# Recurrence stage of a two-block network: each head group's Gram, inverse and scan steps issued by a readiness rule, without fill products, with half of the masks on another engine

## The chip, the cores and the metric

The kernel runs on one NeuronCore of a Trainium2 chip. The core has a matrix engine (TensorE, PE in the rows; PEld is its weight load), a vector engine (VectorE, DVE), an activation engine (ScalarE, ACT), a general engine (GpSimd, POOL), and a DMA issuer (SyncE, SP). Each engine runs its own queue in order; semaphores join them. The metric is the device time in microseconds (us), lower is better; one profiled execution gives the trace.

## The reference, cut to what matters

A first block (conformer mixer and conv FFN) is followed by two layers with FFNs; the first of these layers mixes with a delta-rule recurrence (RWKV-7) over 256 positions, 12 heads of 64 channels. The change is in that mixer alone.

```python
def rwkv7_mix(z_in, mu, w0, w_up, a0, a_up, g_up, k_k, k_a, r_k, lnx_g, lnx_b):
    z = token_shift(z_in, mu)              # p + (prev - p) * mu
    ...
    def step(state, inp):
        r_t, w_t, k_t, v_t, kk_t, b_t = inp
        sa = jnp.einsum('bhij,bhj->bhi', state, kk_t)
        state = (state * w_t[:, :, None, :] - sa[..., :, None] * b_t[..., None, :]
                 + v_t[..., :, None] * k_t[..., None, :])
        return state, jnp.einsum('bhij,bhj->bhi', state, r_t)
    ...
    out = ((out - m) * lax.rsqrt(var + LNX_EPS)).reshape(bsz, seq, c) * lnx_g + lnx_b
    bonus = jnp.sum(r * k * r_k, axis=-1, keepdims=True) * v
    y = (out + bonus.reshape(bsz, seq, c)) * g
```

## The kernel before, in words

Weights stream through a ring: SP loads `wraw`, ACT rounds it to a high part `whi` (line 226), DVE takes the low part `wlo` (line 235), and PE multiplies by both. Layers of the network follow one another on PE with little between them.

The class `Rwkv` works in two parts. `project` (line 1441) computes the projections on PE while side tasks prepare decays and keys; a planner (`weave`) orders its steps by costs written in the code. `shifted` (line 1427) applies the token shift to a projection in PSUM by two DVE instructions, the first into a padded tile `mpad`, the second adding the scaled projection: it is called 18 times on projections of the groups and twice at the start. The last projections are the values `v` (`aa`), two column blocks for each of three head groups (4 heads each).

`groups` (line 1630) then treats the three head groups g = 0, 1, 2 in a fixed order, written out by loops:

- *Gram*: for each g and q (two halves), 16 products of keys with queries go to two PSUM banks (line 1667), and DVE multiplies each bank (128x512) by a mask into `G` (line 1671); then for each g three opening steps on DVE make the first inverse factors: `Y` (line 1677, twice), `Z` (1679), `D` (1680, a transpose).
- *Sides*: for each g, v is turned by 8 products with the identity (line 1688, copied by ACT into `vu`, 1690), the keys `kb` are turned by 8 transposes (line 1695, copied by ACT back, 1696), POOL multiplies the bonus by v (`ys`, 1699) and ACT adds a bias (1701).
- *Inverse*: five levels; at each level one set of 16 64x64 products for each g (helper `each`, line 1711) goes to `Y` by a DVE mask (1718), then a second set for each g goes to `D` (1726) and by a transpose to `Z` (1727); at the last level to `Z` alone (1730). `each` ends by calling `idle(0.22)`, which issues two fill products (line 1294, a 128x256 product of the current weight with itself, result unused).
- *Scan*: four chunks c of 64 positions. For each chunk and each g: products into `sc` (`xp`, lines 1746 and 1749), a DVE copy `xs` (1751), products with `Z` (`up`, 1756), results to `vu` by ACT (1758) and DVE (1759), products into `sc` again (`sp`, 1771) from which DVE makes the next state `S` in four instructions (1777 or 1781), with ACT scaling the old state (`sd`, 1768), and the output products `op` (1786, 1790). Each (c, g) ends with two fill products (line 1294).

The PSUM banks come in turn from two pools of three (`ps`): a bank is given out again when its readers are done. After the scan, `hnorm` normalizes the outputs: ACT and DVE copy `op` to `D` (1799 to 1801), products with a centering matrix (1813), two weight products, and 24 products of 2 columns (1822) between them.

The functions that the change touches, with the lines of the profile:

Of the kernel before, what the change touches and what calls it, by code (L numbers as in the profile page):

```python
# [8 lines left out]
F32 = mybir.dt.float32  # L9
# [1383 lines left out]
class Rwkv(Mixer):  # L1393
# [6 lines left out]
    def run(self, li):  # L1400
        b = self.b
        self.n_ps = 0
        self.ready = {}
# [36 lines left out]
    def project(self):  # L1440
        nc, b, mp = self.nc, self.b, self.mp
        self.omm = mp.tile([P, 20], F32, name="omm")
# [6 lines left out]
        self.mpad = [mp.tile([P, T + 1], F32, name=f"mpad{i}") for i in range(4)]  # L1449
        self.n_pad = 0  # L1450
        for t in self.mpad:
            nc.vector.memset(t[:, 0:1], 0.0)
# [13 lines left out]
        self.n_lora, self.n_prep, self.n_val = 0, 0, 0  # L1466
# [20 lines left out]
        for g in range(3):  # L1487
# [8 lines left out]
            self.n_val += 1  # L1496
# [132 lines left out]

    def groups(self):  # L1630

# [3 lines left out]
        ident = b.k("ident")  # L1635
        R = range(3)
        kof, bof = (0, HD), (HD, 0)
        rows = [slice(bof[q], bof[q] + HD) for q in range(2)]
# [7 lines left out]
        G = [gp.tile([P, 2, 2, 4, P], F32, name="G", bufs=2) for _ in range(2)]  # L1646
        G += tiles("G", [2, 2, 4, P], 1)
        Z, D, Y = (tiles(n, [8, HD]) for n in "ZDY")
        vu = tiles("vu", [2, 4, 2, HD])
        for t in vu:  # L1650
            for q in range(2):
                nc.gpsimd.memset(t[rows[q], q], 0.0)
# [3 lines left out]

        mg = b.k("maskg").unsqueeze(1).to_broadcast([P, 4, P])
        for g in R:  # L1660
            ar, kb, _ = self.ready[g]
            for q in range(2):
                gm = [self.ps().rearrange("p (c f) -> p c f", c=4) for _ in range(2)]
                for c in range(4):
                    for h in range(2):
                        r = slice(h * HD, h * HD + HD)
                        mm(gm[h][:, c, :], lhsT=kb[r, 4 * q + c].rearrange("p a t -> p (a t)"),
                           rhs=ar[r, 4 * q + c].rearrange("p a t -> p (a t)"), start=True, stop=True,
                           skip_group_check=True)
                for h in range(2):  # L1670
                    tt(out=G[g][:, q, h], in0=gm[h], in1=mg, op=ALU.mult)

            odd = slice(1, HD, 2)
            zo = Z[g][:, :, odd]
            for q in range(2):
                r = rows[q]
                tt(out=Y[g][r, :, 0:HD // 2], in0=G[g][r, q, :, :, odd].rearrange("p h c t -> p (h c) t"),
                   in1=b.k("m1neg")[r, odd].unsqueeze(1).to_broadcast([HD, 8, HD // 2]), op=ALU.mult)
            tt(out=zo, in0=zo, in1=Y[g][:, :, 0:HD // 2], op=ALU.add)
            nc.vector.transpose(out=D[g], in_=Z[g])  # L1680

        for g in R:
            zv = self.aa[:, 2 * g:2 * g + 2, :]
            vp = [self.ps().rearrange("p (c f) -> p c f", c=4) for _ in range(2)]
            for q in range(2):
                k = slice(kof[q], kof[q] + HD)
                for c in range(4):
                    mm(vp[q][k, c, :], lhsT=zv[:, q, c * HD:c * HD + HD], rhs=ident, start=True,
                       stop=True, skip_group_check=True)
                nc.scalar.copy(out=vu[g][k, q].rearrange("p c h f -> p c (h f)"), in_=vp[q][k])  # L1690
            kbt = self.ready[g][1].rearrange("p i a t -> p i (a t)")
            for q in range(2):
                tp = self.ps()
                for c in range(4):
                    nc.tensor.transpose(tp[:, c * P:c * P + P], in_=kbt[:, 4 * q + c], identity=ident)
                nc.scalar.copy(out=kbt[:, 4 * q:4 * q + 4].rearrange("p c f -> p (c f)"), in_=tp)

            bon = self.sgw[:, 2 * g:2 * g + 2, :]
            nc.gpsimd.tensor_tensor(out=bon, in0=bon, in1=zv, op=ALU.mult)
            for q in range(2):  # L1700
                nc.scalar.activation(out=bon[:, q, :], in_=bon[:, q, :], func=AF.Identity,
                                     bias=b.vec("rwkv_lnx_b_2", 2 * g + q))
        self.b.mark("inv")

        def each(f):

            o = self.ps().rearrange("p (i t) -> p i t", i=8)
            for i in range(8):
                for q in range(2):
                    lhsT, rhs = f(rows[q], q, i)  # L1710
                    mm(o[rows[q], i, :], lhsT=lhsT, rhs=rhs, start=True, stop=True,  # L1711
                       skip_group_check=True)
            self.idle(self.FILL)
            return o
        for s in LEVELS:
            for g in R:
                yp = each(lambda r, q, i: (G[g][r, q, i // 4, i % 4, 0:HD], D[g][r, i, :]))
                tt(out=Y[g], in0=yp, in1=b.k(f"low{s}").unsqueeze(1).to_broadcast([P, 8, HD]),
                   op=ALU.mult)
            for g in R:  # L1720
                if s < 32:
                    dp = each(lambda r, q, i: (Z[g][r, i, :], Y[g][r, i, :]))

                    def low(t):
                        return t.rearrange("p i (a z s) -> p i a z s", z=2, s=s)[:, :, :, 0, :]
                    tt(out=low(D[g]), in0=low(D[g]), in1=low(dp), op=ALU.subtract)
                    nc.vector.transpose(out=Z[g], in_=D[g])
                else:
                    dp = each(lambda r, q, i: (Y[g][r, i, :], Z[g][r, i, :]))
                    tt(out=Z[g], in0=Z[g], in1=dp, op=ALU.subtract)  # L1730
        S = [tiles(f"S{i}", [2, 2, HD]) for i in range(2)]
        for t in S[0] + S[1]:
            nc.gpsimd.memset(t, 0.0)
        self.b.mark("scan")

# [333 lines left out]
```

## Time and profile before

| | us |
|---|---|
| median of 3 runs | 1512.58 (1511.94 to 1513.09) |
| profiled execution, its own time | 1513.66 |
| its span, first to last instruction | 1511.9 |
| PE busy in the span | 1455.1 (96%) |
| DVE busy | 1076.0 (71%) |
| ACT busy | 832.4 (55%) |
| POOL busy | 103.3 (7%) |

The time lies 1.8 us above the span. PE is busy almost throughout, but its busy time counts fill products and the modelled ends of pipelined products, so a stretch has to be read by the order and starts of its instructions. The recurrence stage lies from 659.4 us to 754.7 us. The stretches named below, from the start of the span: projections to 659.4, Gram and sides to 678.3, inverse to 723.7, scan to 754.7, then hnorm.

### The profile page before, as it was taken

Reading aid. Unit: us, or ns where it says so; the run is one execution under the profiler, and the core shown is the slowest. Engines: PE = TensorE matmul, PEld = TensorE weight load, DVE = VectorE, ACT = ScalarE, POOL = GpSimd, SP = SyncE. Lnnn points to the kernel's source line nnn. Section 1 sums busy time; section 2 is a strip of 40 time slices with the busy share of each in tenths; the row PEclk is TensorE's granted clock in tenths of the full one; section 3 lists DMA queues with packets and bytes.
Section 4 is the critical chain, followed back from the end, with each engine's and each line's share of the span. In section 5 each row is a group of like instructions: output and inputs, shape, how many; then the busy total and the mean of one; then the engine's idle time right before and its main releaser. Section 6 shows DMA issues by size and latency. Waiting matters only on the chain.

```text
span 1511.9 us, 26295 instructions
## 1 busy us (share of the span) xinstructions
PE 1455.1 (96%) x10821; PEld 1300.6 (86%) x10821; DVE 1076.0 (71%) x1701; ACT 832.4 (55%) x1447; POOL 103.3 (7%) x84
## 2 busy tenths in 40 slices
PE   8888899999999999989999999999999999999997
PEld 7867799988888888888888888888888888888886
DVE  8897788884877658985568776577766655687753
ACT  6797476684655536630246555356553576465542
POOL 1110100000000010130010000100002011100010
PEclk9999899999999999999999999999999999999998
DMA  9775345564455453320024555535555332265540
GB/s 380 277 256 195 137 171 192 195 229 175 167 195 195 181 182 133 112 85 3 2 84 148 203 185 190 195 125 209 195 195 184 132 112 90 106 223 191 185 182 28
DMA packets 39146, 250.39 MB, mean 166 GB/s; under 512 B 4337, under 2 KB 4849, under 8 KB 12274
## 3 DMA queue, kind: packets, MB, share of 16 engines
q1 hardware_dynamic: 38594, 247.60, 45.1%
q8 instruction: 85, 1.39, 0.4%
q10 hardware_dynamic: 432, 1.11, 0.3%
q14 instruction: 35, 0.29, 0.1%
HBM read 247.65 MB, written 1.05 MB: 164 GB/s over the span
## 4 chain that ended last, share of the span: by engine, by line
PE 82%; DVE 12%; ACT 4%; issue 2%; DMA 1%; POOL 0%; DVEq 0%; ACTq 0%; POOLq 0%
PE acc L370 26%; PE acc L358 15%; PE gu L358 7%; PE gu L370 7%; PE gu L363 4%; PE gu L364 3%; DVE wlo L235 2%; PE r L1711 2%; PE acc L412 2%; DVE mraw L595 2%; PE st L1219 1%; PE gu L1294 1%; DVE ys L555 1%; PE gu L346 1%; ACT whi L226 1%
## 5 line engine op out<-in xcount | busy, mean ns | idle before, releaser
L235 DVE TENSOR_TENSOR wlo<-wraw,whi 128x1024 fp32r<-128x1024 f32 x416 | 524.2, 1270 | 42.3 <-ACT whi L226 40.1
L226 ACT CAST whi<-wraw 128x1024 fp32r<-128x1024 f32 x416 | 427.2, 1046 | 29.7 <-PE acc L364 7.4
L370 PE MATMUL acc<-hx,whi 128*128 128x512 f32 x880 | 310.8, 398 | 0.0
L358 PE MATMUL acc<-xx,wlo 128*128 128x256 f32 x1088 | 292.8, 284 | 2.9 <-ACT xx L561 1.6
L370 PE MATMUL acc<-xx,whi 128*128 128x512 f32 x832 | 289.6, 390 | 0.0
L358 PE MATMUL gu<-xx,wlo 128*128 128x256 f32 x992 | 278.8, 281 | 0.0
L358 PE MATMUL acc<-hx,wlo 128*128 128x256 f32 x880 | 247.4, 281 | 0.0
L358 PEld LDWEIGHTS acc<-xx,wlo 128*128 128x128 f32 x1088 | 201.2, 190 | 8.5 <-ACT xx L561 4.4
L370 PEld LDWEIGHTS acc<-hx,whi 128*128 128x128 f32 x880 | 165.3, 188 | 40.6
L358 PEld LDWEIGHTS gu<-xx,wlo 128*128 128x128 f32 x992 | 187.6, 189 | 0.2
L370 PEld LDWEIGHTS acc<-xx,whi 128*128 128x128 f32 x832 | 156.2, 188 | 32.7
L358 PEld LDWEIGHTS acc<-hx,wlo 128*128 128x128 f32 x880 | 166.1, 189 | 0.0
L363 PE MATMUL gu<-xx,whi 128*128 128x256 f32 x544 | 158.3, 291 | 2.3 <-ACT u L747 2.3
L370 PE MATMUL gu<-xx,whi 128*128 128x512 f32 x448 | 156.5, 390 | 0.0
L364 PE MATMUL gu<-xx,whi 128*128 128x256 f32 x544 | 152.6, 281 | 0.0
L1179 ACT ACTIVATE ys<-ys 128x256 f32<-128x256 f32 (+1 forms) x66 | 28.6, 437 | 157.5 <-DVE ys L1102 140.6
L363 PEld LDWEIGHTS gu<-xx,whi 128*128 128x128 f32 x544 | 103.0, 189 | 11.2 <-issue 8.4
L364 PEld LDWEIGHTS gu<-xx,whi 128*128 128x128 f32 x544 | 103.1, 189 | 0.7 <-issue 0.7
L370 PEld LDWEIGHTS gu<-xx,whi 128*128 128x128 f32 x448 | 84.1, 188 | 17.7
L1100 DVE SCALAR_TENSOR_TENSOR ys<-xr,acc 128x256 f32<-128x256 f32 x32 | 13.5, 421 | 95.0 <-PE acc L370 95.0
L1196 POOL TENSOR_TENSOR nsum<-ys 128x512 f32<-128x512 f32 (+1 forms) x9 | 13.2, 1466 | 988.2 <-PE acc L370 623.3
L722 ACT COPY lows<-acc 128x256 f32<-128x256 f32 x60 | 22.4, 374 | 103.9 <-PE acc L370 103.8
(352 smaller groups left out, 2274.8 us busy)
## 6 DMA issues: line engine op xcount, KB each, us to landing
wraw<-in_w SPq DMA_DIRECT2D x208, 1024.0 KB, 4.8
mraw<-in_mod SPq DMA_DIRECT2D x48, 512.0 KB, 5.6
xr<-in_x SPq DMA_DIRECT2D x2, 512.0 KB, 4.5
m<-in_mem SPq DMA_DIRECT2D x1, 1024.0 KB, 8.1
out<-xr SPq DMA_DIRECT2D x3, 256.0 KB, 2.2
cst<-in_consts SPq DMA_DIRECT2D x1, 546.0 KB
lora<-in_lora ACTq DMA_DIRECT2D x1, 384.0 KB, 3.4
lora_g<-in_lora ACTq DMA_DIRECT2D x1, 384.0 KB, 4.0
```

The costliest lines, as they stand in the source:

```text
L226: b.nc.scalar.copy(out=hi, in_=raw)
L235: b.nc.vector.tensor_tensor(out=lo, in0=raw, in1=hi.bitcast(F32), op=ALU.subtract)
L346: self.nc.tensor.matmul(ps[:, 0, :], lhsT=w[0][:, 0:P], rhs=w[0][:, 0:T], start=True, stop=True, skip_group_check=True)
L358: self.nc.tensor.matmul(out, lhsT=wl, rhs=x[:, 0, :], start=start, stop=False, skip_group_check=True)
L363: mm(out, lhsT=wh, rhs=x[:, 0, :], start=start, stop=False, skip_group_check=True)
L364: mm(out, lhsT=wh, rhs=x[:, 1, :], start=False, stop=False, skip_group_check=True)
L370: self.nc.tensor.matmul(bank, lhsT=wh, rhs=x, start=False, stop=stop, skip_group_check=True)
L412: self.nc.tensor.matmul(bank, lhsT=wh[:, c], rhs=x[:, k], start=False, stop=k == KD - 1, skip_group_check=True)
L595: self.nc.vector.tensor_tensor(out=raw, in0=raw, in1=self.cact, op=ALU.mult)
L722: nc.scalar.copy(out=lows[:, 1, :], in_=banks[1][:, 1, :])
L1179: b.nc.scalar.activation(out=b.ys[:, k0:k1, 1, :], in_=y, func=AF.Square)
L1711: mm(o[rows[q], i, :], lhsT=lhsT, rhs=rhs, start=True, stop=True, skip_group_check=True)
```

## The change: what it does

The three groups no longer advance in lockstep. A generator `recurrence(g)` holds the whole chain of a group; `rotate` walks the three chains by costs written in the code, always taking the group that would be ready first, and takes side steps (`sides`, now another generator: keys before values) where no group is ready. The fill products of `each` and of the scan are gone. `G` is split into two tiles: `E` (`GE`, columns the inverse reads) is masked by DVE, 128x256 from PSUM; `F` (`GR`, columns that only the outputs read) is copied by ACT and masked in place by POOL, 128x256. `shifted` uses one ACT and one DVE instruction, without `mpad`. The shift of group 2's values is put off from the projections to `sides(2)`. Once the first group scans, all product banks come from one pool of three (`bank`), the other three hold the outputs. The arithmetic on the elements is the same.

```diff
     def shifted(self, z, ps, mu):
-        m = self.mpad[self.n_pad % 4]
-        self.n_pad += 1
-        nc.vector.tensor_scalar(out=m[:, 1:], in0=ps, scalar1=b.vec("rwkv_mu_2", mu), scalar2=None,
-                                op0=ALU.mult)
-        nc.vector.scalar_tensor_tensor(out=z, in0=ps, scalar=self.omm[:, mu:mu + 1], in1=m[:, :T],
-                                       op0=ALU.mult, op1=ALU.add)
+        nc.scalar.activation(out=z, in_=ps, func=AF.Copy, scale=self.omm[:, mu:mu + 1])
+        nc.vector.scalar_tensor_tensor(out=z[:, 1:], in0=ps[:, :T - 1], scalar=b.vec("rwkv_mu_2", mu),
+                                       in1=z[:, 1:], op0=ALU.mult, op1=ALU.add)
...
+            if g == 2:
+                self.late = gv
+                continue
...
+    def rotate(self, gens, fillers):
+        now = dve = 0.0
+        ready = [0.0 for _ in gens]
+        live = list(range(len(gens)))
+        while live:
+            i = min(live, key=lambda i: (max(ready[i], now), i))
+            step = None if ready[i] > now + 0.1 and fillers else next(gens[i], False)
...
+            pe, ve, more = step
+            now = max(now, ready[i]) + pe
+            ready[i] = now + more
+            if ve:
+                dve = max(dve, now + 0.25) + ve
+                ready[i] = dve + more + 0.1
...
+    def bank(self):
+        if not self.scanning:
+            return self.ps()
+        return self.pr.tile([P, 512], F32, name="r", tag="r")
...
+    def sides(self, g):
+        while g not in self.grams:
+            yield None
+        for q in range(2):
+            tp = self.bank()
+            for c in range(4):
+                nc.tensor.transpose(tp[:, c * P:c * P + P], in_=kbt[:, 4 * q + c], identity=ident)
+            nc.scalar.copy(out=kbt[:, 4 * q:4 * q + 4].rearrange("p c f -> p (c f)"), in_=tp)
+            yield 0.6
+        if g == 2:
+            for q in range(2):
+                self.shifted(zv[:, q, :], self.late[:, q, :], 12 + 2 * g + q)
...
+        nc.gpsimd.tensor_tensor(out=bon, in0=bon, in1=zv, op=ALU.mult)
...
+    def recurrence(self, g):
...
             for h in range(2):
-                    tt(out=G[g][:, q, h], in0=gm[h], in1=mg, op=ALU.mult)
+                tt(out=E[:, q, h], in0=gm[h][:, :, 0:HD], in1=me, op=ALU.mult)
+                nc.scalar.copy(out=F[:, q, h], in_=gm[h][:, :, HD:])
+                nc.gpsimd.tensor_tensor(out=F[:, q, h], in0=F[:, q, h], in1=mr, op=ALU.mult)
+            yield 0.95, 1.4, 0.0
...
-            self.idle(self.FILL)
             return o
...
         for c in range(4):
...
-                self.idle(self.FILL)
+            yield 1.2, 0.0, 0.1
```

PE at the passage from the Gram products to the first two rounds of the inverse, before (`r<-head,ys` are the value turns, `r<-head,kb` the key turns, `gu<-whi` the fills):

```order
L1667 MATMUL r<-ar,kb 128x128 x48
L1688 MATMUL r<-head,ys 64x128 x8
L1695 MATMUL r<-head,kb 128x128 x8
L1688 MATMUL r<-head,ys 64x128 x8
L1695 MATMUL r<-head,kb 128x128 x8
L1688 MATMUL r<-head,ys 64x128 x8
L1695 MATMUL r<-head,kb 128x128 x8
L1711 MATMUL r<-D,G 64x64 x16
L1294 MATMUL gu<-whi 128x256 x2
```

The same passage of the changed kernel, also on PE (1672 are the key turns, 1683 the value turns, 1737 the inverse):

```order
L1711 MATMUL r<-ar,kb 128x128 x48
L1672 MATMUL r<-head,kb 128x128 x8
L1683 MATMUL r<-head,ys 64x128 x8
L1672 MATMUL r<-head,kb 128x128 x8
L1683 MATMUL r<-head,ys 64x128 x4
L1737 MATMUL r<-D,GE_6944 64x64 x16
L1683 MATMUL r<-head,ys 64x128 x4
L1737 MATMUL r<-D,GE_6945 64x64 x16
L1672 MATMUL r<-head,kb 128x128 x4
L1737 MATMUL r<-D,GE_6946 64x64 x16
L1737 MATMUL r<-Y,Z 64x64 x48
```

The first set of the inverse now stands after the sides of group 0 and most of those of group 1; a quarter of the turns lies among the first sets, the rest of group 2's turns has moved past the inverse, and no fill stands between sets.

DVE over the same passage, before:

```order
L1671 TENSOR_TENSOR G<-r,cst 128x512 x4
L1677 TENSOR_TENSOR Y<-G,cst 64x8x32 x2
L1679 TENSOR_TENSOR Z<-Z,Y 128x256
L1680 STREAM_TRANSPOSE D<-Z 128x512
L1671 TENSOR_TENSOR G<-r,cst 128x512 x4
L1677 TENSOR_TENSOR Y<-G,cst 64x8x32 x2
```

and after:

```order
L1715 TENSOR_TENSOR GE_6944<-r,cst 128x256 x2
L1715 TENSOR_TENSOR GE_6945<-r,cst 128x256 x2
L1715 TENSOR_TENSOR GE_6946<-r,cst 128x256 x2
L1715 TENSOR_TENSOR GE_6944<-r,cst 128x256 x2
L1715 TENSOR_TENSOR GE_6945<-r,cst 128x256 x2
L1715 TENSOR_TENSOR GE_6946<-r,cst 128x256 x2
L1725 TENSOR_TENSOR Y<-GE_6944,cst 64x8x32 x2
L1727 TENSOR_TENSOR Z<-Z,Y 128x256
L1728 STREAM_TRANSPOSE D<-Z 128x512
L1725 TENSOR_TENSOR Y<-GE_6945,cst 64x8x32 x2
```

All twelve masks (half as wide) now come before the first opening step, the first half of each group ahead of the second halves; before, the four masks and the opening steps of one group stood together.

PE at the entry to the scan in the changed kernel (1777 is `xp`, 1783 `up`, 1797 `sp`, 1816 `op`):

```order
L1777 MATMUL sc<-vu,GE_6944 64x64 x4
L1737 MATMUL r<-Z,Y 64x64 x16
L1783 MATMUL sc<-xs,Z 64x64 x4
L1777 MATMUL sc<-vu,GE_6945 64x64 x4
L1672 MATMUL r<-head,kb 128x128 x4
L1683 MATMUL r<-head,ys 64x128 x4
L1797 MATMUL sc<-vu,kb 64x64 x4
L1816 MATMUL op<-GR_6947,vu 64x64 x4
```

Before, the three groups' `xp` stood in one row of 12 products, then the three `up`, then `sp` and `op` group by group with two fills behind each; now group 0 enters alone and group 2's last turns stand between its `up` and its `sp`. At the end of the scan on PE, the rows of group 2's last chunk (its last `op` pair, which reads like the one shown, follows):

```order
L1774 MATMUL sc<-S_6976,ar 64x128
L1777 MATMUL sc<-vu,GE_6946 64x64 x2
L1783 MATMUL sc<-xs,Z 64x64 x4
L1812 MATMUL op<-ar,S_6976 128x64
L1816 MATMUL op<-GR_6949,vu 64x64 x2
```

Of its last chunk no other group's product stands between the copies, which before had the other two groups' products beside them.

## Rows read from the trace of the kernel before

**Rows 1.** Windows: stretch, length; PE, PEld, DVE, ACT, POOL busy (x count); clock; DMA, GB/s

```profile
575.00:659.40 84.40, 83.96 (x607) 73.76 (x605) 76.56 (x152) 50.41 (x97) 14.00 (x14) 1.00 0.37 135
659.40:678.30 18.90, 15.11 (x169) 12.77 (x168) 15.89 (x29) 6.62 (x14) 2.78 (x8) 1.00 0.16 57
678.30:723.70 45.40, 45.40 (x1021) 39.24 (x1020) 25.65 (x42) 2.35 (x5) 0.00 (x0) 1.00 0.01 3
723.70:754.60 30.90, 30.23 (x455) 25.25 (x454) 17.67 (x62) 7.49 (x25) 0.00 (x0) 1.00 0.01 2
762.00:769.00 7.00, 7.00 (x36) 7.00 (x37) 2.87 (x8) 1.39 (x3) 0.00 (x0) 0.54 0.42 150
```

**Rows 2.** Timeline, Gram and sides: start, us, engine, line, operation, count, [idle before, releaser]

```profile
659.36 2.95 PE L1667 MATMUL r<-ar,kb 64*128 64x128 f32 x48
662.23 2.47 DVE L1671 TENSOR_TENSOR G<-r,cst 128x512 f32<-128x512 f32 x4
664.73 0.87 DVE L1677 TENSOR_TENSOR Y<-G,cst 64x256 f32<-64x256 f32 x2
...
667.51 1.75 PE L1667 MATMUL r<-ar,kb 64*128 64x128 f32 x16 [1.60 <-DVE G L1671]
...
675.77 1.58 PE L1688 MATMUL r<-head,ys 128*64 128x128 f32 x16
677.28 1.09 PE L1695 MATMUL r<-head,kb 128*128 128x128 f32 x8
```

**Rows 3.** Timeline, inverse, PE: first set, two fills, second set

```profile
678.31 1.15 PE L1711 MATMUL r<-D,G 64*64 64x64 f32 x32
679.38 0.50 PE L1294 MATMUL gu<-whi 128*128 128x256 f32 x2
679.82 1.15 PE L1711 MATMUL r<-D,G 64*64 64x64 f32 x32
```

**Rows 4.** Groups by line and shape, 659 to 755: count, busy us, mean ns, idle before

```profile
L1718 DVE TENSOR_TENSOR Y<-r,cst 128x512 f32<-128x512 f32 x15 | 10.4, 691 | 13.1 <-PE r L1711 13.1
L1727 DVE STREAM_TRANSPOSE Z<-D 128x512 f32<-128x512 f32 x12 | 8.5, 711 | 0.4
L1726 DVE TENSOR_TENSOR D<-D,r 128x256 f32<-128x256 f32 x12 | 5.1, 421 | 6.1 <-PE r L1711 6.1
L1696 ACT COPY kb<-r 128x512 f32<-128x512 f32 x6 | 3.3, 588 | 1.3 <-PE r L1695 1.2
```

**Rows 5.** Timeline, scan: the second chunk's last `xs`, then group 0's and 1's steps

```profile
731.00 0.29 DVE L1751 COPY xs<-sc 128x128 f32<-128x128 f32 x1 [0.29 <-PE sc L1749]
731.39 0.74 ACT L1758 ACTIVATE vu<-sc 64x128 f32<-64x128 f32 x3 [5.55 <-PE sc L1756]
731.69 0.75 DVE L1759 TENSOR_SCALAR vu<-sc 64x128 f32<-64x128 f32 x3 [0.40 <-ACT vu L1758]
...
732.60 1.18 DVE L1777 SCALAR_TENSOR_TENSOR S<-sc,pc,sd 64x64 f32<-64x64 f32 x4 [0.16 <-ACT sd L1768]
```

**Rows 6.** Timeline, POOL and DVE, where POOL masks 128x256 in a later layer

```profile
1206.05 2.42 POOL L2016 TENSOR_TENSOR e<-e,sbc 128x256 f32<-128x256 f32 x2 [34.01 <-DVE e L2014]
...
1206.35 3.20 DVE L235 TENSOR_TENSOR wlo<-wraw,whi 128x1024 fp32r<-128x1024 f32 x2
...
1217.80 1.43 POOL L2016 TENSOR_TENSOR e<-e,sbc 128x256 f32<-128x256 f32 x2 [9.33 <-DVE e L2014]
```

**Rows 7.** Timeline, hnorm, PE: before the clock's fall, and behind it

```profile
759.67 0.28 PE L363 MATMUL acc<-xx,whi 128*128 128x256 f32 x1
759.79 0.28 PE L364 MATMUL acc<-xx,whi 128*128 128x256 f32 x1
...
760.37 3.09 PE L1822 MATMUL cs<-cst,Y 128*128 128x2 f32 x24
...
765.61 0.41 PE L364 MATMUL acc<-xx,whi 128*128 128x256 f32 x1
765.82 0.41 PE L358 MATMUL acc<-xx,wlo 128*128 128x256 f32 x1
```

More of the change, by code (lines that the diff above doesn't have):

```diff
@@ L1402, in run @@
         self.n_ps = 0
-        self.ready = {}
+        self.ready, self.grams = {}, set()
         with b.pool("keep") as self.keep:
@@ L1441, in project @@
         nc, b, mp = self.nc, self.b, self.mp
-        self.omm = mp.tile([P, 20], F32, name="omm")
+        self.omm = self.keep.tile([P, 20], F32, name="omm")
         nc.vector.tensor_scalar(out=self.omm, in0=b.vec("rwkv_mu_2", 0, 20), scalar1=-1.0,
@@ L1628, in prepare @@
         yield 0.86, 0.0, 0.0
+    def rotate(self, gens, fillers):
[5 more added lines that the diff above has]
+            step = None if ready[i] > now + 0.1 and fillers else next(gens[i], False)
+            if step is False:
+                live.remove(i)
+                continue
+            if step is None:
+                step = next(fillers[0], False)
+                if step is False:
+                    fillers.pop(0)
+                elif step is None:
+                    now = ready[i]
+                else:
+                    now += step
+                continue
+            pe, ve, more = step
[4 more added lines that the diff above has]
+                ready[i] = dve + more + 0.1
+        for f in fillers:
+            list(f)
@@ new lines, in bank @@
+    def bank(self):
[3 more added lines that the diff above has]
+    def sides(self, g):
+        nc, b, vu = self.nc, self.b, self.vu[g]
+        ident = b.k("ident")
+        while g not in self.grams:
+            yield None
+        kbt = self.ready[g][1].rearrange("p i a t -> p i (a t)")
+        for q in range(2):
[4 more added lines that the diff above has]
+            yield 0.6
+        zv = self.aa[:, 2 * g:2 * g + 2, :]
+        if g == 2:
+            for q in range(2):
+                self.shifted(zv[:, q, :], self.late[:, q, :], 12 + 2 * g + q)
+        for q in range(2):
+            vp = self.bank().rearrange("p (c f) -> p c f", c=4)
+            k = slice(q * HD, q * HD + HD)
+            for c in range(4):
+                nc.tensor.matmul(vp[k, c, :], lhsT=zv[:, q, c * HD:c * HD + HD], rhs=ident, start=True,
+                                 stop=True, skip_group_check=True)
+            nc.scalar.copy(out=vu[k, q].rearrange("p c h f -> p c (h f)"), in_=vp[k])
+            yield 0.9
+        self.sided.add(g)
+        bon = self.sgw[:, 2 * g:2 * g + 2, :]
+        nc.gpsimd.tensor_tensor(out=bon, in0=bon, in1=zv, op=ALU.mult)
+        for q in range(2):
+            nc.scalar.activation(out=bon[:, q, :], in_=bon[:, q, :], func=AF.Identity,
+                                 bias=b.vec("rwkv_lnx_b_2", 2 * g + q))
@@ L1634, in groups @@
         tt = nc.vector.tensor_tensor
-        ident = b.k("ident")
         R = range(3)
-        kof, bof = (0, HD), (HD, 0)
-        rows = [slice(bof[q], bof[q] + HD) for q in range(2)]
         def tiles(name, shape, n=3):
@@ L1645, in groups @@
         gp = gx.enter_context(b.pool("gram", side="right"))
-        G = [gp.tile([P, 2, 2, 4, P], F32, name="G", bufs=2) for _ in range(2)]
-        G += tiles("G", [2, 2, 4, P], 1)
+        self.GE, self.GR = ([gp.tile([P, 2, 2, 4, HD], F32, name=f"{n}{g}") for g in R]
+                            for n in ("GE", "GR"))
         Z, D, Y = (tiles(n, [8, HD]) for n in "ZDY")
-        vu = tiles("vu", [2, 4, 2, HD])
-        for t in vu:
+        self.ZDY = Z, D, Y
+        self.vu = tiles("vu", [2, 4, 2, HD])
@@ L1651, in groups @@
+        for t in self.vu:
             for q in range(2):
-                nc.gpsimd.memset(t[rows[q], q], 0.0)
+                nc.gpsimd.memset(t[HD - q * HD:P - q * HD, q], 0.0)
         for t in Z:
             nc.gpsimd.tensor_copy(out=t, in_=b.k("i64").unsqueeze(1).to_broadcast([P, 8, HD]))
[L1659 to L1670, printed above, removed]
-                    tt(out=G[g][:, q, h], in0=gm[h], in1=mg, op=ALU.mult)
[L1673 to L1712, printed above, removed]
-            self.idle(self.FILL)
[L1714 to L1730, printed above, removed]
@@ L1793, in groups @@
+        self.S = [tiles(f"S{i}", [2, 2, HD]) for i in range(2)]
+        for t in self.S[0] + self.S[1]:
+            nc.gpsimd.memset(t, 0.0)
+        self.sided, self.scanning = set(), False
+        self.op = {}
+        self.rotate([self.recurrence(g) for g in R], [self.sides(g) for g in R])
+        op = [self.op[g] for g in R]
         self.b.mark("hnorm")
```

178 lines of the change are left out of this document (113 added, 65 removed).

## Prediction, made before the changed kernel was run

> **What bounds the kernel now.** I first read the windows by stage [rows 1], to see which engine fills each stretch. The projections are bound by PE: 83.96 of 84.40 us busy, while DVE has 7.8 us and ACT 34 us to spare. So the DVE time that `shifted` gives up there buys nothing. In the inverse PE is busy for all of 45.40 us and DVE for 25.65; in the scan PE for 30.23 of 30.90 and DVE for 17.67. Read alone, that says "bound by TensorE". The next view, PE's timeline of one set [rows 3], says what that busy time is: a set starts at 678.31, its two fills at 679.38, the next set at 679.82. A set is thus 1.07 us of products and 0.44 us of fills whose result nobody reads, and 30 sets of 1.51 us make the 45.4 us. The groups by line [rows 4] show the other side: DVE idles 13.1 us ahead of the 15 masks of line 1718 and 6.1 us ahead of the 12 subtractions, each time released by PE. DVE needs 0.69 us after one kind of set and 0.42 + 0.71 = 1.13 after the other, where two other sets (2.1 us) stand between a group's sets. Three chains in rotation therefore feed PE without the fills.
>
> The Gram stretch differs: PE has 15.11 us of 18.90 busy [rows 1], by records that overlap. Its timeline [rows 2] gives the work: 48 products in 2.95 us, so 96 in 5.9; 16 records of the value turns from 675.77 to 677.28, 1.51 us, and 8 of the key turns to 678.31, 1.03 us, so three sides are 7.6. Work is 13.5 us of 18.95; the rest is waiting, as at 667.51 where PE stood 1.60 us for a mask. The masks only begin at 662.23, 2.9 us behind the products.
>
> **The fills, removed.** 30 pairs in the inverse and 12 in the scan at 0.44 us are 18.5 us of PE's queue [rows 3]. The inverse becomes 30 x 1.08 = 32.4, the scan's PE work 30.23 - 5.3 = 25.0. What stood beside the fills is the question: in the scan's second chunk [rows 5] an `xs` takes 0.29, the three ACT copies 0.74, the three DVE copies 0.75, the four state instructions 1.18. In lockstep two other groups cover them.
>
> **Gram and opening, counted from the first product at 659.36.** PE's 5.9 us of products now run through. A DVE mask of 128x256 is priced by the subtraction of that size, 0.42 [rows 4], so twelve are 5.0 and keep up with PE; the last ends near 6.9. Opening group 0 is `Y` 0.87 [rows 2], `Z` 0.42 and `D` 0.71 [rows 4], 2.0 in all: 8.9. PE meanwhile does turns, which by the order are group 0's 2.54, group 1's keys 1.03 and half its values 0.75, to 10.2. So without disturbance the first set would start at 10.2, bound by PE.
>
> Disturbance comes from POOL. Its twelve masks cost 0.71 each alone (two in 1.43), 1.21 each beside DVE's `wlo` (two in 2.42), and that `wlo` pair took 3.20 [rows 6]. That is 8.5 to 14.5 us of POOL work from about 660.5, over the DVE opening steps, which read SBUF twice as well. This is where the Trainium skill speaks against the change: the page "SBUF — State Buffer", section "Who interferes with whom", says that a DVE instruction with two SBUF inputs and a GpSimd instruction take an exclusive lock, and the second to issue is blocked until the first is through. The rows just named agree, 2.42 against 1.43 us.
>
> I take that each of the three steps Y, Y, Z of group 0 waits one mask of 0.71 and a part of the next group's turns is late with it: first set at 12.5, 2.3 above the free case. The bounds are 10.2 (no collision) and 18.2, where masks take 1.21 each and the opening steps get through only behind the last, 660.5 + 14.5 + 2.0 + hand-offs. I choose nearer the lower end because the masks wait on ACT copies and so come with gaps.
>
> ACT gets the twelve half copies; a 128x512 copy takes 0.59 [rows 4], so one is 0.3 to 0.6 and all are 4 to 7 us, beside 6.62 busy of 18.90 [rows 1]: covered. Behind them ACT's bias step waits for POOL's bonus product, which now queues behind twelve masks; behind that bias stand the next group's key and value copies, and PE waits for their banks. This is why the bound of 18.2 is not wild. The `F` halves are first read by `op` in the scan, over 30 us later, so their own lateness costs nothing. In the projections ACT takes on about 18 x 0.45 = 8 us against 34 spare: 0, at most 0.5 if an ACT cast of weights is held.
>
> **Turns moved.** A quarter of the sides (1.3 us) lies among the first sets, 2.0 (group 2's) at the scan's entry. They cost the same PE time as before, now outside the Gram stretch. For waits among sets I add 0.8: DVE's 30 steps take 15 x 0.69 + 12 x 1.13 + 3 x 0.69, 26 us of 32.4, so only rotation that slips costs.
>
> **Scan stalls.** The groups now enter one by one and end one by one, and PE is in order, so a lone group pays its hand-offs. A lone chunk holds `xs` 0.29, two copies of 0.25, the first state instruction 0.30, and about 0.3 of signals: 1.4 [rows 5]. I count three of them at the entry and two in the tail, 7.0. Late shift: PE's value turn of group 2 stands right behind its key turn, and between them ACT must do the key copy 0.59, its scaling and DVE the second half, at about 0.42 each [rows 4], and signals: 1.9. So 8.9 in all; the bounds are 3 (others cover nearly all) and 16 (every chunk of the twelve pays about 1.2, plus 1.9).
>
> **Sum.** 12.5 + 32.4 + 1.3 + 0.8 + 25.0 + 2.0 + 8.9 = 82.9, against 18.95 + 45.39 + 30.95 = 95.3 before: -12.4. The profiled execution took 1513.66, 1.1 above the median of 1512.58, so the median becomes about 1500.
>
> **The clock.** The fills may have had a second use. The granted clock is 1.00 in every window to 754.6, in the Gram stretch too, where PE is not dense. But 24 products of two columns at 760.37 [rows 7] are followed by a window granted 0.54 [rows 1], about the 1.2 GHz level, and there two neighbouring products are 0.21 us apart instead of 0.12 [rows 7]. In the changed kernel the inverse stays a dense row of products, as in the projections; the thin places are the entry and the tail of the scan. If the fall of 762 comes some us earlier or later, 3 us move in either direction; this is in the range.
>
> **The rivals.** *B, the fills held the clock (slower).* Without them the sets run at the low level through the inverse: 32.4 x (0.21/0.117 - 1), about +26, so some 1526. It decides from about 15 us of time lost, some 28 us of the 82.9 at the low level. For it speaks the fall after 760; against it that the Gram stretch, with PE waits of 1.60, kept 1.00. Chance 0.06.
>
> *C, POOL's masks shut DVE out.* The first set starts at 18.2 and not 12.5: +5.7, about 1506. For it: [rows 6], and the ACT bias step queued behind POOL. Against: DVE's masks read PSUM, and only the opening steps collide. The page's lock rule, applied to each of these steps, gives this rival. Chance 0.15.
>
> *D, everything is covered.* First set at 10.2, no waits among sets, stalls of 3: 10.2 + 32.4 + 1.3 + 25.0 + 2.0 + 3 = 73.9, so -21.4, about 1491. For it: DVE has 20 us idle in the inverse. Chance 0.13.
>
> *E, the fills only stood in waits.* PE would then wait wherever a fill stood, and the change, though it does what it says, brings nothing: 1512.6. Against it stands the DVE idle time of [rows 4], which shows DVE waiting for PE. Chance 0.05.
>
> **How the numbers follow.** The forecast, 1500, has the rest, 0.61. Below 0.2% (3 us) no change can be told here. Faster: forecast, C and D, 0.89; within: E, 0.05; slower: B, 0.06. The range leaves out B, E and the far ends of C and D: 1490.5 (D's 1491 and the clock's small share) to 1508 (C with 2 us of a shifted clock fall).
>
> **What would show it.** Right: the sets of the inverse follow one another at 1.08 us, 30 in 33 to 35 us; the first set starts 11 to 14 us behind the first Gram product; PE idle in the scan sums to 7 to 11 us, with the largest single wait ahead of group 2's value turns; granted clock 1.00 up to hnorm. Wrong: idle of PE inside the inverse above 3 us (E, or a planner's costs that do not meet the chip's), opening steps of DVE stretched or late with POOL busy beside them (C), a granted clock of 0.5 between 670 and 745 (B), PE idle in the scan under 4 us (D).

## The result, and the profile after

The changed kernel takes 1492.64 us (median of 4 runs, 1491.20 to 1495.15) against 1512.26 for the kernel before: ratio 0.9876, interval 0.9856 to 0.9895. That is 19.6 us faster, where 12.4 were forecast; the time lies in the range that was given. In a later run, beside the kernel before without fills, it took 1495.55 (0.9901, interval 0.9884 to 0.9917).

The windows by stage of the changed kernel answer to [rows 1] (stretch, length; busy time of PE, PEld, DVE, ACT, POOL; granted clock; DMA share, GB/s). The first runs from the first Gram product to the first set of the inverse, the second to the first scan product, the third to the first product of hnorm:

```profile
658.45:668.58 10.13, 10.13 (x137) 9.34 (x137) 8.02 (x17) 6.26 (x16) 8.03 (x11) 1.00 0.31 105
668.58:699.88 31.30, 29.25 (x942) 28.62 (x941) 28.15 (x48) 4.53 (x9) 3.81 (x4) 1.00 0.02 4
699.88:734.96 35.08, 30.88 (x487) 26.26 (x484) 19.51 (x65) 11.09 (x32) 1.26 (x1) 1.00 0.01 2
```

Cut in the same way, the kernel before has 95.6 in all, now 76.5:

```profile
659.36:678.31 18.95, 15.16 (x170) 12.82 (x169) 15.94 (x29) 6.63 (x14) 2.82 (x8) 1.00 0.16 57
678.31:723.71 45.40, 45.40 (x1022) 39.24 (x1021) 25.66 (x42) 2.34 (x5) 0.00 (x0) 1.00 0.01 3
723.71:754.99 31.28, 30.61 (x457) 25.59 (x457) 17.66 (x62) 7.71 (x26) 0.00 (x0) 1.00 0.01 2
```

The Gram stretch gave 8.8, of which about 3.3 are turns that moved into the two stretches behind it, and the inverse 14.1; the scan took 3.8 back. In the inverse DVE is now nearly as busy as PE, 28.15 of 31.30. The projections, from their first product of line 363, grew from 77.73 (581.63 to 659.36) to 78.82 (579.63 to 658.45).

PE's timeline of the changed kernel answers to [rows 3] (start, us, engine, line, operation, count, [idle before, releaser]):

```profile
668.58 1.15 PE L1737 MATMUL r<-D,GE 64*64 64x64 f32 x32
669.66 1.09 PE L1683 MATMUL r<-head,ys 128*64 128x128 f32 x8
672.15 1.15 PE L1737 MATMUL r<-D,GE 64*64 64x64 f32 x32 [1.41 <-DVE D L1728]
673.23 0.66 PE L1672 MATMUL r<-head,kb 128*128 128x128 f32 x4
674.53 1.15 PE L1737 MATMUL r<-D,GE 64*64 64x64 f32 x32 [0.64 <-DVE D L1728]
675.49 3.00 PE L1737 MATMUL r<-Y,Z 64*64 64x64 f32 x96
678.29 3.00 PE L1737 MATMUL r<-D,GE 64*64 64x64 f32 x96
```

Ahead of the second and third first sets PE waits for the opening steps. From there three sets start every 2.80 us: 0.933 for a set, not 1.08. In the scan the waits over 0.3 us, on the same view, are these:

```profile
704.52 0.95 PE L1683 MATMUL r<-head,ys 128*64 128x128 f32 x7 [1.66 <-DVE ys L1431]
...
720.35 0.40 PE L1774 MATMUL sc<-S,ar 128*64 128x128 f32 x2 [0.66 <-DVE S L1807]
...
730.36 0.45 PE L1797 MATMUL sc<-vu,kb 128*64 128x64 f32 x8 [0.69 <-DVE vu L1786]
...
733.25 0.45 PE L1783 MATMUL sc<-xs,Z 64*64 64x64 f32 x8 [0.38 <-DVE xs L1779]
```

The first is the late shift of group 2's values; the last two stand in group 2's lone chunks.

### The profile page after: what moved, and what is told of

Same layout as the page of the kernel before. It is cut to its first block, busy times and chain, and to the rows that moved or that the text cites. A ratio compares the mean times of both kernels' runs of the same rounds, so it can differ in the third digit from the quotient of the medians.

```text
span 1491.5 us, 26146 instructions
## 1 busy us (share of the span) xinstructions
PE 1435.5 (96%) x10737; PEld 1288.1 (86%) x10737; DVE 1064.8 (71%) x1677; ACT 843.4 (57%) x1479; POOL 109.2 (7%) x96
## 4 chain that ended last, share of the span: by engine, by line
PE 82%; DVE 11%; ACT 5%; issue 2%; POOL 0%; DVEq 0%; ACTq 0%; POOLq 0%
PE acc L370 26%; PE acc L358 15%; PE gu L358 7%; PE gu L370 7%; PE gu L363 4%; PE gu L364 4%; PE r L1737 2%; PE acc L412 2%; DVE wlo L235 2%; PE st L1219 1%; DVE mraw L595 1%; ACT whi L226 1%; PE gu L346 1%; DVE ys L555 1%; PE acc L862 1%
```

## The experiments

Stretches are cut as above: Gram, inverse, scan, and their sum.

### The fills put back into the changed kernel, and taken out of the kernel before

In the changed kernel, at the end of `each` and of each group-chunk of the scan:

```diff
+            self.idle(self.FILL)
             return o
...
+            self.idle(self.FILL)
             yield 1.2, 0.0, 0.1
```

In the kernel before:

```diff
-    FILL = 0.22
+    FILL = 0.0
```

> The changed kernel with its fill pairs put back: two fill products behind each of the 30 sets of the inverse and behind each of the 12 group-chunks of the scan; all else as changed. In the trace of the changed kernel three sets follow each other in 2.80 us, 0.933 each, where the kernel before needed 1.514 for a set with its pair: theory 'full price', a pair costs 0.58 and not the 0.44 between its start and the next product, because the switch from the small products to the fills and back also costs. It expects the sets' pitch back at 1.51, the inverse 17 us longer less the 2 us of waits that fills now stand in, the scan 12 x 0.5 = 6 longer less 2 to 4 of waits: +18 to +22 us on the changed kernel, 1511 to 1515. Rival 'pair is 0.44', some other thing made the sets faster: sets at 0.933 + 0.44 = 1.37, +18.5 less 5 = +13, about 1506. Rival 'fills stood in waits': +5 or less, under 1498.

> The kernel before with the fill products taken out and nothing else: the groups stay in lockstep, all masks stay on DVE. Theory 'fills are the gain': DVE needs 3 x (0.69 + 1.13) = 5.5 us in a level and six sets at 0.933 are 5.6, so lockstep covers the steps too; the inverse falls from 45.4 to 28 to 30, the scan from 31 to 24 to 26, the Gram stretch stays at 19: -22 us, about 1490, as fast as the changed kernel, and the readiness order and the split masks add nothing in the sum because what they save in the Gram stretch they lose in the scan. Rival 'the order is needed': without readiness PE waits for DVE among the sets, 1 us or more in each level and in each chunk; -10 to -14 us, 1498 to 1502. Rival 'the clock': granted clock of 0.5 somewhere between 680 and 745, slower than the kernel before or near it.

With fills the changed kernel takes 1516.69 (1.0034, 1.0016 to 1.0051): a little slower than the kernel before, and 1.7 above the range expected. On PE a set with its pair is back at 1.51 (682.08 to 683.60):

```profile
682.08 0.51 PE L1294 MATMUL gu<-whi 128*128 128x256 f32 x2
682.52 1.15 PE L1737 MATMUL r<-D,GE 64*64 64x64 f32 x32
683.60 0.51 PE L1294 MATMUL gu<-whi 128*128 128x256 f32 x2
```

So a pair costs 1.51 - 0.93 = 0.58, as 'full price' had it; the sum of the three stretches rose by 20.3, to 96.8. Its rival of 0.44 falls.

The kernel before without fills takes 1490.81 (0.9860, 0.9832 to 0.9888), no slower than the changed kernel. Its windows:

```profile
662.71:683.27 20.56, 17.99 (x170) 15.50 (x169) 16.01 (x29) 6.64 (x14) 2.88 (x8) 0.83 0.16 53
683.27:711.41 28.14, 28.14 (x961) 28.07 (x960) 23.60 (x41) 2.34 (x5) 0.00 (x0) 1.00 0.02 4
711.41:738.58 27.17, 25.53 (x437) 21.95 (x433) 17.70 (x62) 7.48 (x25) 0.00 (x0) 1.00 0.01 3
```

The inverse falls to 28.14 = 30 x 0.938 with PE busy throughout and no wait: in lockstep, too, DVE keeps up. The scan falls by 4.1, 0.34 for each of 12 pairs. The Gram stretch is 1.6 longer than before at a granted clock of 0.83; the first fill of the kernel before stands behind this stretch (679.38 in [rows 3]), so its code up to there is the same and the missing fills are not the cause. The readiness order is not needed to cover the steps; the rival that it is falls.

### One fill in place of two

```diff
-    FILL = 0.22
+    FILL = 0.11
```

> The kernel before with one fill product where there were two, nothing else. A set is 0.933 us without fills and 1.514 with a pair. Theory 'a switch and two products': 0.22 for a fill product (the pair starts 0.44 ahead of the next set) and 0.14 for the switch between the kinds of products, whatever their number; a set with one fill is 0.933 + 0.14 + 0.22 = 1.29, the inverse 30 x 1.29 = 38.8. Rival 'price by the piece', 0.29 each: 1.22, inverse 36.7. Rival 'fills hide waits that come back without them' is ruled out if the sets stay evenly spaced. Time between 1498 and 1502.

```profile
681.41 0.39 PE L1294 MATMUL gu<-whi 128*128 128x256 f32 x1
681.73 1.15 PE L1711 MATMUL r<-D,G 64*64 64x64 f32 x32
682.80 0.38 PE L1294 MATMUL gu<-whi 128*128 128x256 f32 x1
```

A set with one fill is 1.39 (681.41 to 682.80), the inverse 41.80; the time 1507.12 (0.9976, 0.9963 to 0.9989). Neither form holds. None, one and two fills make 0.93, 1.39 and 1.51: the first costs 0.46 and the second 0.12, the distance of neighbouring projection products in [rows 7]. So 0.34 of a pair's 0.58 comes with the passage from the inverse's products to the fill and back, for one fill as for two.

### GpSimd's work held behind the opening steps

First by order alone: the masks and bonus products are issued behind the third group's opening, the first two groups' bias steps at the scan's entry.

```diff
-                nc.gpsimd.tensor_tensor(out=F[:, q, h], in0=F[:, q, h], in1=mr, op=ALU.mult)
+                self.held.append((F[:, q, h], mr))
...
+        if self.opened == 3:
+            for f, m in self.held:
+                nc.gpsimd.tensor_tensor(out=f, in0=f, in1=m, op=ALU.mult)
```

> The changed kernel with all of GpSimd's work of this stage (twelve masks, the bonus products) issued behind the third group's opening steps, and the two first groups' bias steps on ACT at the scan's entry. Theory 'collision': the opening steps on DVE go back from 3.2, 3.7 and 2.2 us to 2.0 each, the waits of 1.41 and 0.64 us ahead of the second and third first sets go to under 0.3, the time falls by 1.5 to 2, to about 1491; the sets keep their pitch of 0.933. Rival 'DVE's own queue': the openings are late because DVE does twelve masks first; they keep 3 us each and the waits stay within 0.5 of what they are. Rival 'GpSimd now collides with the inverse': the steps of the inverse on DVE (0.69, 0.42, 0.71) grow and PE waits there, no gain or a loss.

This tested nothing of GpSimd: its queue holds nothing ahead of the masks, so they ran when ACT had copied, from 661.23 as from 660.55 in the changed kernel, and PE waited 1.42 and 0.63. It took 1494.88 (0.9886, 0.9863 to 0.9910). Only the bias steps on ACT moved, and that brought no gain. So the masks were made to wait for data:

```diff
+            mr = self.mp.tile([P, HD], F32, name="mr", bufs=1)
+            nc.vector.tensor_copy(out=mr, in_=b.k("maskg")[:, HD:])
+            for f in self.held:
+                nc.gpsimd.tensor_tensor(out=f, in0=f, in1=mr.unsqueeze(1).to_broadcast([P, 4, HD]),
+                                        op=ALU.mult)
```

> The changed kernel with GpSimd's twelve masks made to wait: their mask operand is a small copy that DVE makes behind the third group's opening steps, so GpSimd cannot run beside them; bonus products and bias steps as in the run with GpSimd's work issued later, which left GpSimd's time as it was since nothing made it wait (its twelve masks ran from 661.23 there, from 660.55 in the changed kernel). Theory 'collision': the opening steps go from 3.2, 3.7 and 2.2 us to 2.0 each, the waits of 1.41 and 0.64 ahead of the second and third first sets go under 0.3, first Gram product to the end of the scan falls from 76.5 to about 74.5. Rival 'collision only moves': the masks then stand beside the first levels of the inverse, whose DVE steps (0.69, 0.42, 0.71) grow, and PE waits 1.5 or more there; no gain. Rival 'no collision': opening steps keep their length, waits unchanged.

Group 0's opening on DVE and GpSimd's rows beside it, first in the changed kernel:

```profile
664.89 1.67 DVE L1725 TENSOR_TENSOR Y<-GE,cst 64x256 f32<-64x256 f32 x2
666.66 0.77 DVE L1727 TENSOR_TENSOR Z<-Z,Y 128x256 f32<-128x256 f32 x1
...
660.55 9.03 POOL L1717 TENSOR_TENSOR GR<-GR,cst 128x256 f32<-128x256 f32 x12 [6.23 <-ACT GR L1716]
```

and then with the masks held:

```profile
665.95 0.87 DVE L1735 TENSOR_TENSOR Y<-GE,cst 64x256 f32<-64x256 f32 x2
666.92 0.43 DVE L1737 TENSOR_TENSOR Z<-Z,Y 128x256 f32<-128x256 f32 x1
...
672.64 8.27 POOL L1744 TENSOR_TENSOR GR<-GR,mr 128x256 f32<-128x256 f32 x12 [17.28 <-DVE mr L1742]
```

`Y` and `Z` fall from 1.67 and 0.77 to 0.87 and 0.43; both waits ahead of the first sets are gone, and the inverse is 29.11. 'Collision' holds: DVE's steps with two SBUF inputs had taken twice as long beside GpSimd. The inverse's own steps, none of which has two inputs from SBUF (`D` and `Y` read PSUM and one SBUF tile, `Z` is a transpose of one tile), kept their length beside the masks (`D` 0.42, `Z` 0.71). The Trainium skill's page "SBUF — State Buffer", section "Who interferes with whom", has it that a DVE instruction with two SBUF inputs contends with a GpSimd instruction that reads SBUF, and one with at most one SBUF input, outside the modes that use two ports, does not. These rows agree with it. The three stretches sum to 75.4, where 74.5 was expected. The whole time shows no gain, 1493.68 (0.9889, 0.9865 to 0.9913); this trace has a granted clock of 0.95 in the scan, which took 36.13.

### The early shift, and the old shift

The early one, in `project` (its counterpart in `sides` is taken out):

```diff
-            if g == 2:
-                self.late = gv
-                continue
```

The old one, in `shifted`, in place of its two instructions:

```diff
+        nc.vector.tensor_scalar(out=m[:, 1:], in0=ps, scalar1=b.vec("rwkv_mu_2", mu), scalar2=None,
+                                op0=ALU.mult)
+        nc.vector.scalar_tensor_tensor(out=z, in0=ps, scalar=self.omm[:, mu:mu + 1], in1=m[:, :T],
+                                       op0=ALU.mult, op1=ALU.add)
```

> The changed kernel with the shift of group 2's values done in the projections as for the other two groups, not in the sides at the scan's entry. Theory 'late shift costs a stall': the wait of 1.66 us ahead of group 2's value turns falls under 0.4, and the time falls by 1.2 to 1.7, to about 1491. Rival 'it only moves': DVE and ACT start the masks 0.5 to 1.0 later, so the first set of the inverse comes that much later (10.13 us behind the first Gram product now, 10.6 to 11.1 then), and the time stays within 0.7 of the changed kernel.

> The changed kernel with the old form of the token shift (two DVE instructions and the padded tile), all else as changed. From the first projection product to the first Gram product the kernel before takes 77.73 us and the changed kernel 78.82, also 78.8 in the three variants of it so far and 77.72 in the kernel before without fills. Theory 'the new shift costs 1.1 us in the projections' (its ACT instructions queue between casts of weights, or move the planner's steps): 77.7 again. Rival 'the other edits in the projections do it' (late shift, no count of values): 78.8 stays; the early shift left it at 78.75. On the whole time -1 or 0, which the time alone can hardly tell.

Early: 1497.55 (0.9900, 0.9873 to 0.9927). The wait at the scan's entry fell from 1.66 to 0.67, but the masks on DVE began later (2.10 behind the first Gram product, not 1.19), the first set came at 10.75 instead of 10.13, and among the first sets PE now waits 0.47, 0.69 and 1.73; the three stretches sum to 77.1, not less than 76.5. By the stretches the rival holds: it only moves. The time lies outside the rival's 0.7, though; 3.15 us of what the profiled execution is longer lie ahead of the projections (582.78 against 579.63), in code that is the same.

Old: 1493.39 (0.9885, 0.9862 to 0.9907), and the projections take 77.76 (581.80 to 659.56). 'The new shift costs 1.1' holds. The order of PE's products is the same in both; in the changed kernel two rows of PE's timeline wait for ACT, which with the old shift they do not:

```profile
610.78 1.27 PE L1567 MATMUL r<-cst,sqk 128*128 128x2 f32 x8 [0.16 <-ACT sqk L1562]
...
641.61 1.08 PE L1374 MATMUL r<-mpt,memv 128*64 128x256 f32 x4 [0.35 <-ACT mpt L1369]
```

The two waits are 0.51, but at these two places the changed kernel falls behind by the whole 1.1. The first row starts 0.33 later than with the old shift, counted from the first projection product, and its eight products take 1.27 instead of 0.95; the second row adds 0.40.

### The scan in lockstep

```diff
         self.rotate([self.recurrence(g) for g in R], [self.sides(g) for g in R])
+        gens = [self.scan(g) for g in R]
+        for _ in range(12):
+            for g in R:
+                next(gens[g])
```

> The changed kernel with the scan in lockstep: the three chains run by readiness through the inverse, then all sides are finished (with the late shift and its wait of 1.66), then chunk by chunk the three groups take each step side by side, as before, without fills. Theory 'readiness loses in the scan what it gains in the Gram stretch': from the first scan product to hnorm the kernel before without fills takes 27.2 (with 3.4 us of it at the low clock), the changed one 35.1 with 2.0 of turns in it; so here about 26, and 3.7 of sides and wait move ahead of it: first Gram product to hnorm 76.5 -> 71 to 72, time 1487 to 1489. Rival 'the scan of the changed kernel is bound by something else' (three product banks, GpSimd's halves): 33 or more for the scan, no gain.

1491.65 (0.9873, 0.9849 to 0.9898), which the time alone does not tell from the changed kernel; the three stretches sum to 74.9, where 71 to 72 were expected. The window of the scan alone:

```profile
709.84:737.17 27.33, 25.76 (x434) 22.13 (x432) 17.20 (x61) 8.94 (x28) 0.30 (x1) 1.00 0.01 3
```

The changed kernel's 35.08 holds a last set of the inverse (0.98), group 2's turns (2.0) and the late shift's wait (1.66), which here stand ahead of the scan: 30.4 against 27.3, so going one by one costs 3.1. That part of the theory holds, at a smaller size: "about 26" took the 27.2 of the kernel before without fills to hold time at the low clock, but its scan's window shows 1.00. The sum fell by 1.6 only: the late shift's wait stayed, and from 690 on three sets took up to 3.07 instead of 2.80, at a granted clock of 1.00. The cause of that last part, about 1 us, is open.

### The parts together

GpSimd held, old shift in the projections, lockstep scan, and group 2's late shift issued on ACT and DVE behind its second level; then, in a second kernel, the bias steps moved away from the scan's entry.

```diff
+                if g == 2 and s == LEVELS[1]:
+                    for q in range(2):
+                        z = self.aa[:, 4 + q, :]
...
```

The second kernel against the first:

```diff
-        self.biases(R)
+                if g == 2 and s == LEVELS[3]:
+                    self.biases([0, 1])
...
+            if k == 5:
+                self.biases([2])
```

> All of it together: GpSimd's masks behind the opening steps, old token shift in the projections, lockstep scan, and group 2's late shift issued on ACT and DVE behind its second level, so that PE does not wait for it. If the parts add up: projections 77.7, first Gram product to hnorm 76.5 - 2 - 5 - 1.7 = 67 to 69, time 1482 to 1486. If DVE is the bound of the inverse once its steps stand close (28.45 us busy of 31.7 in the changed kernel) the late shift and the lost overlap give 2 to 3 back: 70 to 72, 1486 to 1489.

> The combined kernel, in which six bias steps stood on ACT ahead of the scan's first copies (2.50 us, and PE waited 1.85 for the copy of DVE behind them), with these steps moved: the first two groups' behind the fourth level of the inverse, the third's into the scan. Theory 'ACT's queue': the wait of 1.85 falls under 0.4, first Gram product to hnorm falls from 72.1 to 70 to 70.5, time 1484 to 1487. Rival 'DVE's first states are the limit there' (eleven of them back to back, 3.29 us): the wait only moves to the second chunk's products, 72 stays.

Combined: 1488.00 (0.9839, 0.9818 to 0.9860). A wait of its own making stood in the scan, on PE and on ACT:

```profile
707.36 0.45 PE L1828 MATMUL sc<-vu,kb 128*64 128x64 f32 x8 [1.85 <-DVE vu L1817]
...
704.19 2.50 ACT L1704 ACTIVATE ys<-ys,vecs 128x256 f32<-128x256 f32 x6
```

The six bias steps held ACT's copies of `vu`, behind which DVE's stand. With them moved that wait is gone (0.22 is left) and the time is 1485.35 (0.9830, 0.9816 to 0.9845), the fastest of all; 'ACT's queue' holds. The steps of the first two groups ran from 683.18, long before the fourth level, since nothing stood ahead of them on ACT. Its windows:

```profile
657.51:667.64 10.13, 10.13 (x137) 9.34 (x136) 7.86 (x20) 7.34 (x18) 0.00 (x0) 1.00 0.29 105
667.64:700.60 32.96, 32.26 (x994) 31.42 (x993) 27.55 (x50) 5.06 (x11) 12.03 (x15) 1.00 0.02 3
700.60:728.01 27.41, 25.79 (x434) 22.15 (x432) 17.21 (x61) 9.15 (x29) 0.00 (x0) 1.00 0.01 3
```

70.5 in sum, where 67 to 69 would have been the parts added: the scan is 27.4 and not 26, and a wait of 0.70 came in where the late shift takes DVE's time. It is still 4 us less than the 74.5 that the kernel before without fills takes in the trace below: with the scan in lockstep, the new order of the Gram stretch is worth something.

### Fills out, against the whole change, on one chip

Both kernels as above, with no edit.

> The changed kernel once more, beside the kernel before without fills on the same chip, because the two lay 1.8 us apart with intervals that overlap, and the low clock stood in different stretches of their traces. Theory 'the fills are the whole gain': 1491 to 1495, first Gram product to hnorm 76.5, and not faster than the other.

> The kernel before without fills once more, on the same chip as the changed kernel. Where its trace shows no low clock between the first Gram product and hnorm: Gram stretch 18.95, inverse 28.1, scan 25.5 to 26, together 73, against 76.5 of the changed kernel; projections 77.7 against 78.8. Theory 'the fills are the whole gain and the rest costs some': 1488 to 1492, 2 to 5 under the changed kernel. Rival 'the order holds the clock': this kernel has the low clock in the stretch again, 75.5 or more, and the two times are equal.

1495.55 (0.9901, 0.9884 to 0.9917) for the change, 1491.26 (0.9875, 0.9859 to 0.9892) for the kernel before without fills. Twice the change is the slower, by 1.8 and 4.3 us. The first time the intervals overlap widely, the second time a little, and there each of the change's four times (from 1494.00) lies above each of the other's (to 1493.20). The windows of the kernel without fills:

```profile
659.63:678.74 19.11, 16.51 (x169) 14.27 (x168) 16.04 (x29) 6.47 (x14) 2.89 (x8) 0.91 0.16 56
678.74:706.89 28.15, 28.15 (x962) 28.08 (x961) 23.58 (x41) 2.40 (x5) 0.00 (x0) 1.00 0.02 4
706.89:734.12 27.23, 25.59 (x436) 21.97 (x432) 17.70 (x62) 7.48 (x25) 0.00 (x0) 1.00 0.01 3
```

Against the changed kernel's first trace, Gram is 19.11 to 10.13, the inverse 28.15 to 31.30, the scan 27.23 to 35.08, the projections 77.77 to 78.82; the sum over all four is 152.3 to 155.3. The low clock in the Gram stretch came again, as the rival 'the order holds the clock' had it, but the times are not equal, and the rival falls. With fills in both kernels the change is slower (1516.69 to 1511.22), without fills in both it is slower too: the fills are the whole gain. The scan of the change in this second trace was lengthened by the clock, which first fell behind the wait at the scan's entry:

```profile
700.68:738.32 37.64, 33.68 (x487) 28.79 (x484) 19.52 (x65) 11.08 (x32) 1.26 (x1) 0.89 0.01 2
...
704.00:706.00 2.00, 0.67 (x6) 0.70 (x7) 0.76 (x2) 1.14 (x3) 0.00 (x0) 1.00 0.00 0
706.00:710.00 4.00, 4.00 (x47) 3.77 (x46) 1.92 (x7) 0.85 (x2) 1.26 (x1) 0.57 0.02 4
```

## Why the prediction was right in sign and short in size

**Fills.** The step that failed on size is the reading of [rows 3]. A set was priced from its start to the start of its fills, 1.07, and the pair from there to the next set, 0.44. But a pair costs 0.58, and the missing 0.14 lay in the 1.07. 30 x 1.08 = 32.4 should have been 30 x 0.933 = 28.0: 4.4 us of the 7.2 by which the forecast was short. No set stood without fills in the rows of before, but the pitch of the records inside a set would have told it. In the trace of the kernel before, the first 6 records of the set at 679.82 take 0.39 and the first 20 take 0.80, so 0.41 / 14 = 0.029 each, 0.94 for the 32 of a set; the changed kernel has 2.80 / 96 = 0.029.

**First set.** 12.5 was predicted, 10.13 came, PE-bound as in the free case of 10.2: 2.4 us. The collision with GpSimd was real, and for group 0 its opening took 3.3 instead of 2.0, 1.3 more where 2.3 were put; the turns covered it, and they were not late. It came out one place later, as 2.05 us of waits ahead of the second and third sets, where 0.8 was put for waits: 1.25 us the other way. So rival C's mechanism is there, at 2 us in place of 5.7.

**Scan.** 35.9 was predicted for work, turns and stalls; the windows of inverse and scan together, 66.4, less 28.0 for the sets, 1.3 for turns and 2.05 for waits, leave 35.1. The late shift's stall was 1.66 (1.9 predicted). By subtraction, 35.1 - 25.0 - 2.0, the stalls are 8.1; the timeline's waits sum to 4.2, under the 7 to 11 that were to show. So the sum came out for a reason that is in part another: PE's busy time for the scan's own products is 27.9 (30.88 less 0.98 and 2.0), where lockstep without fills has 25.5, and why the same products take 2.4 more one group after another was not tried. The prediction saw that a lone group pays its hand-offs. Its own terms give 18.95 + 32.4 + 25.7, about 77, for lockstep without fills, against 82.9 for the change; it never set the two side by side, and so did not say that the order gives back more than the Gram stretch brings.

**Projections.** "0, at most 0.5" for `shifted` was wrong: it costs 1.1, at two places where PE's products wait for ACT. ACT's 50 of 84 us busy hid that the shift's scaling stands ahead of copies and squares on ACT for which single products wait.

**The rest.** The forecast's sum of the recurrence was 82.9, to 754.65; 76.5 was measured, 6.4 less. The projections' 1.1 goes against that. The remaining 2.0 of the trace lies ahead of the projections (579.63 against 581.63), in code that did not change; over the profiles here this start lies between 578.55 and 584.99, so 2.0 is taken as no effect of the change. Of the turns, 8 of 48 stand among the first sets, a sixth and not a quarter; the 1.3 us put for them is right.

**Rivals.** B did not come: granted clock 1.00 from 658.45 to 734.96, and 1.00 in the inverse of every kernel without fills here. E is refuted by both fill runs. D's time of 1491 was close, but by other terms: its stalls of 3 did not come, its first set of 10.2 did. The condition "PE idle in the inverse above 3 us" was not met (2.05). Of the signs for "right", the largest wait ahead of group 2's value turns came, and the clock of 1.00 in the first trace; the pitch of 1.08, the first set at 11 to 14 and the 7 to 11 us of idle time did not. That the time still lies in the range, 2 us above its lower end, is in part luck: D's terms set that end, and the sets of 0.933 that brought the time there were in no term of the range.

## What to carry to other kernels

Before judging a reordering by its total, take out the filler alone: here it was the whole gain, and the reordering on top cost 2 to 4 us while it looked like part of the win. Price a filler from the pitch of the useful work without it, not from its own start to the next product, since the switch there and back costs more than the product. Chains that run by readiness end and begin alone, which cost 3.1 us in this scan; keep independent chains side by side where each step is a hand-off between engines, and use readiness where other work can fill the gap, as in the Gram stretch here. Moving an instruction within a queue that is empty ahead of it moves nothing, as the masks on GpSimd and the bias steps on ACT showed: only a dependency does.

## What the runs showed of the hardware

Going from the fp32 products of 64x64 to one fill of 128x256 and back costs 0.34 us beyond the fill's 0.12. GpSimd's masks doubled DVE steps with two SBUF inputs (0.87 to 1.67, 0.43 to 0.77; 0.43 to 1.31 beside a bonus product), and left steps that read PSUM as they were (twelve masks on DVE 5.22 with them and without). The granted clock fell in the scan of three of the six profiles of kernels without fills whose scan runs by readiness (0.95, 0.89, 0.88, the scan 1.0 to 2.8 us longer than 35.08), and in none of the five with a lockstep scan; these are means of stretches in which part ran at the low level. Each time it first fell behind the thin place at the scan's entry. In the kernel before without fills it fell in the Gram stretch, twice (0.83, 0.91), behind PE's wait of 1.60 for masks; the kernel before had the same wait at 1.00. Why the same code has it in one execution and not in another was not tried. The three profiles of kernels with fills show 1.00 from the first Gram product to hnorm; that the fills hold the clock in the scan is not excluded by so few, but they cost more than the fall (20.3 us against 1.0 to 2.8).
